# Moving the squares' sums, the sample copies and the row transposes at the border between attention and feed-forward

## The chip, the cores and the metric

The kernel runs on one core of one Trainium2 chip. The metric is the time of one execution in microseconds (us) on the device. Five engines work side by side, each through its own instructions in order: PE (matrix products), DVE (elementwise), ACT (activations and copies), POOL (elementwise) and SP (here only issuing transfers). Matrix products go to PSUM, from where ACT or DVE take them.

## The reference, cut to what matters

One decoder layer for two groups of tokens: 1024 prompt tokens and 8 x 4 sample tokens, width 1024, fp32.

```python
x = x + rms_norm(m, norm_g[1])                      # after the token mixer
h = rms_norm(x, norm_g[2])
x = x + rms_norm(mem_attend(h, mem_k, mem_v, *attn_w), norm_g[3])
h = rms_norm(x, norm_g[4])
x = x + rms_norm(swiglu(h, *ffn_w), norm_g[5])      # (silu(h @ w_gate) * (h @ w_up)) @ w_down
```

The border of this text is the third and fourth line: the attention's output projection, its norm (norm 3), the residual sum, and the norm of that (norm 4), from which the gate and up products start.

## The kernel before, in words

Activations are kept transposed: 128 features on the partitions, tokens along the free axis, in tiles of 128 x 2 x 264 (528 elements). Eight tiles (k = 0 to 7) are the 1024 features of one half of the tokens; the halves are called b = 0 and b = 1. Each fp32 operand is split into a high and a low part (ACT copies the high part, DVE subtracts to get the low part), and each product is three matmuls: high x high, high x low, low x high.

**Output projection** (`attn_out`): for a half, eight blocks, one for each 128 output features. A block is 24 pairs of matmuls (`pao`), then ACT squares the result from PSUM (`sq_n`), the square is added to a running sum (`square_sum`, lines 204 to 210), and ACT copies the result out of PSUM with its gain (`mg`, line 979). Only with both done is the block's PSUM tile free; there are three of them.

**Residual and norms** (`tokens_ffn`): a matmul with ones (`os_n`, line 216) adds the squares over the partitions, ACT takes the root (line 223), DVE the inverse (line 224). DVE scales the eight `mg` tiles by it and adds them to the eight residual tiles `xo` (line 81). Those are squared again and summed (`acc_n`), and with the second inverse the normed tiles (`a`, line 1255) are made and split. For b = 0 they are the matrices A11 and A12, for b = 1 DVE makes the sums and differences of a Strassen scheme (AS1 to AS4, A22). In the kernel before, norm 3's squares are added on POOL for both halves, norm 4's on POOL for b = 0 and on DVE for b = 1.

**Rows** (`rows_in`): each residual tile is also needed in row form at the end. PE transposes its four 128x128 pieces into PSUM (`xn`, line 1229), ACT copies them (line 1231) and SP stores them; the eight sample columns are copied to `xsam` by POOL (line 1225).

**Products ahead** (`ahead_pairs`): six pairs of gate and up blocks for b = 0. Each block is two half products of 12 pairs of matmuls (`xA`, line 1308), with A11 and then with A12; between the two ACT copies the first half's result (`p`, line 1330), which is stored. The gate block is activated by ACT (`gA`, line 1336), and DVE multiplies it by the up block. After these come the 11 full pairs.

A scheduler orders the instructions of each engine from the order of the code and its own estimate of time. What is written side by side with `run(...)` alternates, a step of each in turn. Rings of buffers couple the engines: two PSUM tiles for `xn` and `xA` together, eight tiles tagged `co` (`mg`, normed tiles, gates), five tagged `tmp` (squares, row copies, copies of products), two or four for each kind of weight buffer.

Of the kernel before, what the change touches and what calls it, by code (L numbers as in the profile page):

```python
# [12 lines left out]
AF = mybir.ActivationFunctionType  # L13
# [7 lines left out]
KT = 8  # L21
# [21 lines left out]
def decode_step(ctx: ExitStack, tc: tile.TileContext, I, O):  # L43
    nc = tc.nc
    act, dve, pool, pe, sync = nc.scalar, nc.vector, nc.gpsimd, nc.tensor, nc.sync
# [9 lines left out]
    def unit(name, dt=F32, shape=(P, 2, W), tag="act"):  # L55
        return acts.tile(list(shape), dt, tag=tag, bufs=BUFS[tag], name=name)

    def tmp(name, dt=F32, shape=(P, 2, W)):
        return unit(name, dt, shape, "tmp")
# [3 lines left out]
    def mm_tile(name):  # L63

        turn[0] += 1
        third = turn[0] % 3 == 0 and not streams
        return ps.tile([P, 2, 512], F32, tag="pw" if third else "mm", bufs=1 if third else 2, name=name)
# [12 lines left out]
    def tt(out, a, b, op, eng=None):  # L80
        (eng or dve).tensor_tensor(out, a, b, op)  # L81
# [4 lines left out]
    def split_into(hi, lo, x, scale=None, eng=None):  # L86

        if scale is None:
            act.activation(hi, x, AF.Copy)  # L89
            low(eng or dve, lo, x, hi)  # L90
        else:
            act.activation(hi, x, AF.Copy, scale=scale)
            dve.scalar_tensor_tensor(lo, x, scale, hi.bitcast(F32), op0=ALU.mult, op1=ALU.subtract)
# [6 lines left out]
    def run(*gens):  # L100

        gens = [g for g in gens if g is not None]
        while gens:
            gens = [g for g in gens if next(g, END) is not END]

    END = object()
# [53 lines left out]
    def gain(n, k):  # L160
        return gains[:, 8 * n + k: 8 * n + k + 1]
# [42 lines left out]
    def square_sum(acc, x, k, name, eng=None):  # L204
        if k == 0:
            act.activation(acc, x, AF.Square)
        else:
            sq = tmp(f"sq_{name}{k}")
            act.activation(sq, x, AF.Square)  # L209
            tt(acc, acc, sq, ALU.add, eng or pool)  # L210
# [9 lines left out]
    def rsqrt(x, n, name, r):  # L220

        for s, total in enumerate(ones_sum(x, name)):
            act.activation(r[:, s, :], total, AF.Sqrt, scale=1.0 / n, bias=eps_rms)  # L223
        dve.reciprocal(r, r)  # L224
        return r
# [34 lines left out]
    def rtile(name):  # L260
        return tiny.tile([P, 2, W], F32, tag="r", bufs=2, name=f"r_{name}")

    def acc_tile(name):
        return accp.tile([P, 2, W], F32, tag="acc", bufs=2, name=f"acc_{name}")
# [710 lines left out]
    def result(b, n, out, norm, acc):  # L975

        mg = unit(f"mg{norm}{b}{n}", tag="co")
        square_sum(acc, out, n, f"n{norm}{b}")
        act.activation(mg, out, AF.Copy, scale=gain(norm, n))  # L979
        return mg  # L980

# [28 lines left out]
    mgA, mgB = [], []  # L1010
    accA, accB = acc_tile("moA"), acc_tile("moB")
# [178 lines left out]
    xsam = fp.tile([P, KT, 4, NB], F32, name="xsam")  # L1190

    def fa_tile(name, dt=F32):
        return fp.tile([P, 2, W], dt, tag="fa", bufs=24, name=name)
# [19 lines left out]
    def keep(n, kt, x):  # L1213

        fa = n in ("S1", "S2", "S4")
        hi, lo = ((fa_tile if fa else unit)(f"A{n}{kt}{i}", F32R) for i in "hl")
        split_into(hi, lo, x)
        A[n][kt] = (hi, lo)

    xo = [[], []]  # L1220

    def rows_in(b, k):

        x = xo[b][k]
        pool.tensor_copy(xsam[:, k, 2 * b:2 * b + 2, :], x[:, :, 0:8])
        pt = mm_tile(f"xn{b}{k}")[:, 0].rearrange("p (t d) -> p t d", t=4)
        for s in range(2):
            for i in range(2):
                pe.transpose(pt[:, 2 * s + i], x[:, s, 8 + i * P:8 + (i + 1) * P], ident)
        xn = tmp(f"xn{b}{k}_", F32, (P, 4, P))  # L1230
        act.activation(xn, pt, AF.Copy)
        sync.dma_start(xnat[4 * b:4 * b + 4, :, k * P:(k + 1) * P].rearrange("t p d -> p t d"), xn)

    def tokens_ffn(b, mgs, acc):

        r = rsqrt(acc, D, f"n3{b}", rtile(f"n3{b}"))
        acc2 = acc_tile(f"n4{b}")
        yield
        for k in range(KT):
            name = f"xo{b}{k}"  # L1240
            if b and k == 7:
                x = fp.tile([P, 2, W], F32, name=name)
            else:
                x = unit(name) if b and k < 3 else fa_tile(name)
            sync.dma_start(x, xres[b][k])
            tt(mgs[k], mgs[k], r, ALU.mult)
            tt(x, x, mgs[k], ALU.add)
            square_sum(acc2, x, k, f"n4{b}", dve if b else pool)
            xo[b].append(x)
            yield  # L1250
        r2 = rsqrt(acc2, D, f"n4{b}", rtile(f"n4{b}"))

        def normed(k, name):
            t = unit(name, tag="co")
            dve.scalar_tensor_tensor(t, xo[b][k], gain(4, k), r2, op0=ALU.mult, op1=ALU.mult)
            return t

        for kt in range(4):
            if b == 0:
                for n, k in (("11", kt), ("12", kt + 4)):  # L1260
                    t = normed(k, f"a{n}{kt}")
                    keep(n, kt, t)
                    sync.dma_start(hb0[k], t)
            else:
                a11, a12 = (unit(f"b1{i}{kt}", tag="co") for i in range(2))
                sync.dma_start(a11, hb0[kt])
                sync.dma_start(a12, hb0[kt + 4])
                a21, a22 = normed(kt, f"a21{kt}"), normed(kt + 4, f"a22{kt}")
                s3 = unit(f"s3{kt}", tag="co")
                tt(s3, a11, a21, ALU.subtract)  # L1270
                tt(a21, a21, a22, ALU.add)
                tt(a11, a21, a11, ALU.subtract)
                keep("S2", kt, a11)
                keep("S1", kt, a21)
                keep("S3", kt, s3)
                tt(a12, a12, a11, ALU.subtract)
                keep("S4", kt, a12)
                keep("22", kt, a22)
            yield


# [2 lines left out]
    def raw_tile(name, shape):  # L1284
        wturn[0] += 1
        if wturn[0] % 2:
            return ring.tile(list(shape), F32, tag="wst", name=name)
        return fp.tile(list(shape), F32, tag="ww", bufs=2, name=name)
# [14 lines left out]
    def product(out, w, a, first=True):  # L1303
        outs = [out[0], out[1]]
        for kt in range(4):
            for i, (c, x) in enumerate(((0, 0), (0, 1), (1, 0))):
                for o, part in zip(outs, both):
                    pe.matmul(o, lhsT=w[:, c, kt], rhs=part(a[kt][x]), start=first and kt == 0 and i == 0,  # L1308
                              stop=kt == 3 and i == 2, skip_group_check=not first)

    def x_tile(name):
        t = ps.tile([P, 2, 512], F32, tag="mm", bufs=2, name=name)
        return t[:, :, :W], [t[:, 0, :W], t[:, 1, :W]]
# [5 lines left out]
    def ahead_pairs():  # L1319

        for i in range(AHEAD):
            g = None
            for m in range(2):
                src = mats[m][0, :, 256 * i:256 * i + P].rearrange("(k p) n -> p k n", p=P)
                ww = raw_tile(f"wA{i}{m}", (P, KT, P))
                sync.dma_start(ww, src)
                X, xs_ = x_tile(f"xA{i}{m}")
                product(xs_, two_parts(ww[:, 0:4], f"wA{i}{m}a"), A["11"])
                p1 = tmp(f"p1{i}{m}")
                act.activation(p1, X, AF.Copy)  # L1330
                sync.dma_start(p1d[i][m], p1)
                yield
                product(xs_, two_parts(ww[:, 4:8], f"wA{i}{m}b"), A["12"], False)
                if m == 0:
                    g = unit(f"gA{i}", tag="co")
                    act.activation(g, X, AF.Silu)
                else:
                    tt(g, g, X, ALU.mult)
                    sync.dma_start(hidd[2 * i][0], g)
                yield  # L1340
# [69 lines left out]
    mgA, mgB = [], []  # L1410
    accA, accB = acc_tile("aoA"), acc_tile("aoB")
# [6 lines left out]
    run(first)  # L1418
    run(second)
    streams.append(1)  # L1420

    def all_rows():
        for b in range(2):
            for k in range(KT):
                while len(xo[b]) <= k:
                    yield
                rows_in(b, k)
                yield

    run(tokens_ffn(1, mgB, accB), ahead_pairs(), all_rows())  # L1430
    for i in range(PAIRS):
        pair(i)
    streams.clear()
# [87 lines left out]
    for s4 in range(4):  # L1521
        b, s = s4 // 2, s4 % 2
# [44 lines left out]
```

## Time and profile before

| | us |
|---|---|
| median of 3 runs | 1656.31 |
| lowest, highest | 1650.68, 1656.35 |
| the profiled execution | 1651.99 |
| its span | 1650.3 |

Busy time in the profiled execution: PE 1509.9 us (91%), DVE 997.2 (60%), ACT 684.5 (41%), POOL 352.0 (21%). Engine shares are means over stages with different limits; the border lies between about 757 and 980 us. A row of a time-ordered view gives the start, the duration, the engine, the line, the operation with output and inputs, and in brackets the time that the engine stood still just before with the instruction that released it. Several equal instructions in a row are one row (x2, x4), and then the duration is that of all of them.

### The profile page before, as it was taken

The page shows a single profiled execution, that of the slowest core. Times are in us where ns is not written, and L with a number is a line of the kernel's source. Part 1 is how long each engine was busy: PE and PEld are TensorE (multiplying, and loading weights), DVE is VectorE, ACT ScalarE, POOL GpSimd, SP SyncE. Part 2 cuts the span into 40 slices and gives each one's busy share as a digit, 9 for nine tenths or more (in the row PEclk, how much of TensorE's full clock was granted, in tenths as well). Part 3 has the DMA queues.
Part 4 walks back from the last instruction along what each step waited for, and adds up shares of the span by engine and source line. Part 5 has one row for each costly group of instructions (what it writes and reads, how often), then busy time and mean ns, then how long its engine had stood idle before and what let it go on. Part 6 is the DMA issues. An engine that isn't in the chain of part 4 may idle for free. (4 is left out here: it accounts for less than half of the span.)

```text
span 1650.3 us, 29329 instructions
## 1 busy us (share of the span) xinstructions
PE 1509.9 (91%) x11731; PEld 1460.7 (89%) x11731; DVE 997.2 (60%) x1678; ACT 684.5 (41%) x1226; POOL 352.0 (21%) x436
## 2 busy tenths in 40 slices
PE   7998889889999899789958799999999999999995
PEld 5888878889999889679957799999999999999995
DVE  6888786476468845583555857766555533444345
ACT  5444533457554544474444633232333334212122
POOL 1366556330334320051342000000000000000004
PEclk9989989899999999899979989999999999999998
DMA  8422223456244503546335643332222225232124
GB/s 244 148 72 69 64 70 100 137 163 197 71 144 149 175 25 117 156 152 190 88 103 177 198 149 117 117 115 93 84 78 78 69 92 173 91 105 66 52 65 156
DMA packets 216116, 194.33 MB, mean 118 GB/s; under 512 B 21900, under 2 KB 180036, under 8 KB 215972
## 3 DMA queue, kind: packets, MB, share of 16 engines
q1 hardware_dynamic: 215852, 192.30, 37.9%
q8 instruction: 92, 1.51, 0.4%
q14 instruction: 44, 0.36, 0.1%
q10 hardware_dynamic: 128, 0.16, 0.0%
HBM read 146.33 MB, written 46.51 MB: 117 GB/s over the span
## 5 line engine op out<-in xcount | busy, mean ns | idle before, releaser
L1496 POOL COPY ysam<-ya 128x8 f32<-128x8 f32 x32 | 5.6, 192 | 717.9 <-DVE ya L81 717.7
L81 DVE TENSOR_TENSOR ya<-ya,fd 128x528 f32<-128x528 f32 x64 | 45.0, 704 | 105.8 <-PE fd L191 105.8
L191 PE MATMUL pao<-oth,hi_wa 128*128 128x264 f32 x256 | 54.9, 297 | 19.1 <-ACT mg L979 19.1
L176 ACT ACTIVATE hi_wd<-st_wd 128x1024 fp32r<-128x1024 f32 x20 | 21.2, 1060 | 121.5 <-PE fd L191 121.3
L81 DVE TENSOR_TENSOR c<-c,X 128x528 f32<-128x528 f32 x51 | 35.8, 703 | 39.7 <-PE X L1308 39.7
L191 PEld LDWEIGHTS pao<-oth,hi_wa 128*128 128x128 f32 x256 | 42.0, 199 | 19.9 <-ACT mg L979 19.7
L191 PE MATMUL pao<-oth,lo_wa 128*128 128x264 f32 x256 | 54.4, 294 | 0.4 <-DVE lo_wa L84 0.4
L191 PE MATMUL pao<-otl,hi_wa 128*128 128x264 f32 x256 | 54.1, 294 | 0.0
L643 PE MATMUL pcv<-vf,cm 128*128 128x128 f32 x320 | 46.2, 296 | 8.4 <-ACT ob L645 5.0
L643 PEld LDWEIGHTS pcv<-vf,cm 128*128 128x128 f32 x320 | 42.8, 209 | 10.5 <-issue 6.2
L84 DVE TENSOR_TENSOR lo_wa<-st_wa,hi_wa 128x1024 fp32r<-128x1024 f32 x16 | 20.6, 1288 | 47.3 <-ACT hi_wa L176 47.3
L191 PEld LDWEIGHTS pao<-oth,lo_wa 128*128 128x128 f32 x256 | 41.7, 197 | 0.7 <-DVE lo_wa L84 0.6
L191 PEld LDWEIGHTS pao<-otl,hi_wa 128*128 128x128 f32 x256 | 41.8, 198 | 0.1
L84 DVE TENSOR_TENSOR kl<-pkr,kh 128x512 fp32r<-128x512 f32 x32 | 21.9, 690 | 28.8 <-ACT kh L89 28.6
L84 DVE TENSOR_TENSOR lo_wd<-st_wd,hi_wd 128x1024 fp32r<-128x1024 f32 x20 | 24.5, 1225 | 22.9 <-ACT hi_wd L176 19.8
L81 POOL TENSOR_TENSOR acc_n<-acc_n,sq_n 128x528 f32<-128x528 f32 x21 | 29.5, 1406 | 39.6 <-ACT sq_n L209 39.5
L224 DVE RECIPROCAL r_n<-r_n 128x528 f32<-128x528 f32 x8 | 27.6, 3451 | 15.7 <-ACT r_n L223 15.7
L753 DVE TENSOR_TENSOR_SCAN M<-rho,X 128x256 f32<-128x256 f32 x32 | 29.8, 956 | 7.3 <-POOL X L81 7.3
L89 ACT ACTIVATE wc<-t 128x512 fp32r<-128x512 f32 x22 | 13.9, 632 | 47.5 <-PE X L1308 25.4
L645 ACT ACTIVATE ob<-pcv,cbias 128x128 f32<-128x128 f32 x32 | 11.6, 364 | 48.9 <-PE pcv L643 47.8
L81 DVE TENSOR_TENSOR c<-c,c 128x528 f32<-128x528 f32 x45 | 31.6, 702 | 0.1
L89 ACT ACTIVATE kh<-pkr 128x512 fp32r<-128x512 f32 x32 | 18.9, 597 | 30.7 <-PE pkr L1135 28.7
(2045 smaller groups left out, 5726.6 us busy)
## 6 DMA issues: line engine op xcount, KB each, us to landing
hr<-hid SPq DMA_DIRECT2D x44, 264.0 KB
ww<-in_w_gate_dram SPq DMA_DIRECT2D x22, 512.0 KB
ww<-in_w_up_dram SPq DMA_DIRECT2D x22, 512.0 KB
st_wd<-in_w_down_dram SPq DMA_DIRECT2D x20, 512.0 KB
hid<-c SPq DMA_DIRECT2D x38, 264.0 KB
xo<-x SPq DMA_DIRECT2D x32, 264.0 KB
kr<-in_cache_mem_k_dram SPq DMA_DIRECT2D x32, 256.0 KB
st_wo<-in_w_out_dram SPq DMA_DIRECT2D x16, 512.0 KB
```

Of the source, the lines that this page charges most:

```text
L81: (eng or dve).tensor_tensor(out, a, b, op)
L84: eng.tensor_tensor(lo, x, hi.bitcast(F32), ALU.subtract)
L89: act.activation(hi, x, AF.Copy)
L176: act.activation(hi[:, :cols], stv, AF.Copy)
L191: pe.matmul(out, lhsT=a, rhs=part(b), start=first and i == 0, stop=last and i == 2)
L224: dve.reciprocal(r, r)
L643: pe.matmul(o, lhsT=cm[:, d].rearrange("p c t -> p (c t)"), rhs=vf[:, g, 4 - d:CH - d], start=d == 0, stop=d == 4)
L645: act.activation(ob[:, g4], o, AF.Identity, bias=cbias[:, gg:gg + 1])
L753: dve.tensor_tensor_scan(out=M[:, i], data0=rho[:, pair:pair + 1].to_broadcast([P, 256]), data1=X[:, i], initial=0.0, op0=ALU.mult, op1=AL ...
L1496: pool.tensor_copy(ysam[:, n, 2 * b + s, :], yacc[b][n][:, s, 0:8])
```

## The change

Norm 4's squares are added on DVE for both halves, and norm 3's on DVE for the last two blocks of each half. The sample columns are copied by ACT in place of POOL. The row transposes of b = 0 stand ahead of the products, those of b = 1 inside the loop that makes its normed tiles. The products are no longer alternated evenly with the residual and the rows: the residual of b = 1 advances one step for each step of the products, and two steps of products are taken once its eight tiles are done.

```diff
-        square_sum(acc, out, n, f"n{norm}{b}")
+        square_sum(acc, out, n, f"n{norm}{b}", dve if norm == 3 and n > 5 else pool)
...
-        pool.tensor_copy(xsam[:, k, 2 * b:2 * b + 2, :], x[:, :, 0:8])
+        act.activation(xsam[:, k, 2 * b:2 * b + 2, :], x[:, :, 0:8], AF.Copy)
...
-            square_sum(acc2, x, k, f"n4{b}", dve if b else pool)
+            square_sum(acc2, x, k, f"n4{b}", dve)
...
                 keep("22", kt, a22)
+                rows_in(1, kt)
+                rows_in(1, kt + 4)
             yield
...
-    def all_rows():
-        for b in range(2):
-            for k in range(KT):
-                while len(xo[b]) <= k:
-                    yield
-                rows_in(b, k)
-                yield
-
-    run(tokens_ffn(1, mgB, accB), ahead_pairs(), all_rows())
+    for k in range(KT):
+        rows_in(0, k)
+    chain, fill = tokens_ffn(1, mgB, accB), ahead_pairs()
+    for n in range(KT + 5):
+        next(chain, END)
+        for _ in range(2 if n > KT else 1):
+            next(fill, END)
+    run(chain)
+    run(fill)
```

The order of PE at the sum of norm 4's squares of b = 0 (`os_n` from `acc_n`), in the second half's output projection, before:

```order
L191 MATMUL pao_9661<-oth_7975,lo_wa_9658 128x264 x2
L191 MATMUL pao_9661<-oth_7977,hi_wa_9657 128x264 x2
L191 MATMUL pao_9661<-otl_7978,hi_wa_9657 128x264 x2
L216 MATMUL os_n_9527<-acc_n_9238,ones 128x264
L216 MATMUL os_n_9529<-acc_n_9238,ones 128x264
L191 MATMUL pao_9661<-oth_7977,lo_wa_9658 128x264 x2
L191 MATMUL pao_9661<-oth_7979,hi_wa_9657 128x264 x2
```

and with the change:

```order
L191 MATMUL pao_9601<-otl_7978,hi_wa_9597 128x264 x2
L191 MATMUL pao_9601<-oth_7977,lo_wa_9598 128x264 x2
L191 MATMUL pao_9601<-oth_7979,hi_wa_9597 128x264 x2
L191 MATMUL pao_9601<-otl_7980,hi_wa_9597 128x264
L216 MATMUL os_n_9527<-acc_n_9238,ones 128x264
L216 MATMUL os_n_9529<-acc_n_9238,ones 128x264
L191 MATMUL pao_9601<-otl_7980,hi_wa_9597 128x264
L191 MATMUL pao_9601<-oth_7979,lo_wa_9598 128x264 x2
```

The sum moved from the sixth block (9661, after 17 of its 24 pairs) to the fifth (9601, after 19 and a half).

The order of PE where the second half's output projection (`pao_9781` is its last block) meets the first product, before:

```order
L1308 MATMUL xA_9846<-A113l,wA00a 128x264 x2
L1308 MATMUL xA_9846<-A113h,wA00a 128x264 x2
L1229 MATMUL xn_9878<-ident,xo_9239 128x128 x4
L216 MATMUL os_n_9836<-acc_aoB,ones 128x264
L216 MATMUL os_n_9838<-acc_aoB,ones 128x264
L1308 MATMUL xA_9846<-A120h,wA00b 128x264 x2
```

and with the change:

```order
L191 MATMUL pao_9781<-oth_7981,lo_wa_9778 128x264 x2
L1229 MATMUL xn_9836<-ident,xo_9239 128x128 x4
L1229 MATMUL xn_9845<-ident,xo_9244 128x128 x4
L216 MATMUL os_n_9908<-acc_aoB,ones 128x264
L216 MATMUL os_n_9910<-acc_aoB,ones 128x264
L1229 MATMUL xn_9854<-ident,xo_9251 128x128 x4
L1229 MATMUL xn_9863<-ident,xo_9258 128x128 x4
L1229 MATMUL xn_9872<-ident,xo_9265 128x128 x4
L1229 MATMUL xn_9881<-ident,xo_9272 128x128 x4
L1229 MATMUL xn_9890<-ident,xo_9279 128x128 x4
L1229 MATMUL xn_9899<-ident,xo_9286 128x128 x4
L1310 MATMUL xA_9918<-A110h,wA00a 128x264 x2
```

All eight row transposes of b = 0 and the sum of norm 3's squares of b = 1 (`os_n` from `acc_aoB`) now stand ahead of the first product; before, one transpose stood behind each half product. Behind it the half products of the first two pairs now come as gate, up, gate, up (A11, A11, A12, A12).

On ACT, the copy that frees the fourth block's PSUM tile (`mg_9590`) had only splits of normed tiles ahead of it; before:

```order
L89 ACTIVATE A121h<-a_9555 128x528
L89 ACTIVATE A112h<-a_9562 128x528
L89 ACTIVATE A122h<-a_9569 128x528
L979 ACTIVATE mg_9590<-pao_9477,gains 128x528
L89 ACTIVATE A113h<-a_9576 128x528
```

and with the change:

```order
L89 ACTIVATE A112h<-a_9562 128x528
L89 ACTIVATE A122h<-a_9569 128x528
L89 ACTIVATE wA10a<-wA_10066 128x512
L89 ACTIVATE wA11a<-wA_10142 128x512
L979 ACTIVATE mg_9590<-pao_9477,gains 128x528
L89 ACTIVATE A113h<-a_9576 128x528
```

The two copies of weights of the second pair, which stood three rows further ahead, now stand directly ahead of it.

## Rows read from the trace of the kernel before

**Rows 1.** Busy time by stretch: PE, PEld, DVE, ACT, POOL, granted clock, DMA share, GB/s.

```profile
806.00:873.00 67.00, 47.90 (x351) 47.05 (x350) 40.09 (x46) 29.22 (x47) 25.64 (x21) 0.85 0.32 100
873.00:953.50 80.50, 61.71 (x456) 57.09 (x454) 61.34 (x88) 45.82 (x81) 8.37 (x9) 0.92 0.61 185
...
980.00:1240.00 260.00, 260.00 (x2142) 260.00 (x2142) 168.57 (x261) 85.22 (x141) 0.00 (x0) 1.00 0.34 106
```

**Rows 2.** Waits of PE, 806 to 960: total us, times, longest.

```profile
PE pao L191 <- ACT mg L979: 19.1, 3, 14.1
PE xn L1229 <- ACT gA L1336: 10.2, 2, 6.1
PE xA L1308 <- ACT p L1330: 1.9, 5, 0.8
PE xA L1308 <- ACT xn__10482 L1231: 1.4, 1, 1.4
```

**Rows 3.** PE in order of time at the border.

```profile
805.67 1.05 PE L216 MATMUL os_n<-acc_aoA,ones 128*128 128x264 f32 x4
...
830.04 0.81 PE L191 MATMUL pao<-oth,hi_wa 128*128 128x264 f32 x2 [4.74 <-ACT mg L979]
...
842.57 1.05 PE L216 MATMUL os_n<-acc_n,ones 128*128 128x264 f32 x4
...
859.38 0.81 PE L191 MATMUL pao<-oth,hi_wa 128*128 128x264 f32 x2 [14.06 <-ACT mg L979]
...
872.67 0.41 PE L1308 MATMUL xA<-A110h,wA00a 128*128 128x264 f32 x2
...
875.60 0.60 PE L1229 MATMUL xn<-ident,xo 128*128 128x128 f32 x4
...
951.68 1.12 PE L1229 MATMUL xn<-ident,xo 128*128 128x128 f32 x4 [0.69 <-ACT xn__10637 L1231]
953.48 0.81 PE L1308 MATMUL xA<-A110h,wA40a 128*128 128x264 f32 x2 [0.69 <-ACT xn__10675 L1231]
...
958.44 0.40 PE L1308 MATMUL xA<-A113h,wA40a 128*128 128x264 f32 x2
```

**Rows 4.** ACT in order of time, 815 to 966.

```profile
825.73 0.64 ACT L209 ACTIVATE sq_n<-xo 128x528 f32<-128x528 f32 x1 [2.98 <-POOL acc_n L81]
...
855.07 0.63 ACT L89 ACTIVATE wA10a<-wA 128x512 fp32r<-128x512 f32 x1 [1.52 <-DMA wA<-in_w_gate_dram]
...
858.63 0.70 ACT L979 ACTIVATE mg<-pao,gains 128x528 f32<-128x528 f32 x1
...
887.84 0.64 ACT L206 ACTIVATE acc_n<-xo 128x528 f32<-128x528 f32 x1 [2.78 <-DVE xo L81]
```

**Rows 5.** DVE in order of time, 755 to 966.

```profile
822.75 1.22 DVE L84 TENSOR_TENSOR lo_wa<-st_wa,hi_wa 128x1024 fp32r<-128x1024 f32 x1
...
844.17 3.45 DVE L224 RECIPROCAL r_n<-r_n 128x528 f32<-128x528 f32 x1 [3.48 <-ACT r_n L223]
...
849.63 1.21 DVE L84 TENSOR_TENSOR lo_wa<-st_wa,hi_wa 128x1024 fp32r<-128x1024 f32 x1
...
919.19 3.45 DVE L224 RECIPROCAL r_n<-r_n 128x528 f32<-128x528 f32 x1 [1.96 <-ACT r_n L223]
...
955.28 0.70 DVE L84 TENSOR_TENSOR AS43l<-b,AS43h 128x528 fp32r<-128x528 f32 x1
```

**Rows 6.** POOL by line, 817 to 848: busy us, mean ns, idle before.

```profile
L81 POOL TENSOR_TENSOR acc_n<-acc_n,sq_n 128x528 f32<-128x528 f32 x7 | 9.1, 1306 | 0.1
...
L1225 POOL COPY xsam<-xo 128x16 f32<-128x16 f32 x8 | 7.6, 987 | 13.7 <-DVE xo L81 13.7
```

**Rows 7.** The nearest small copy on ACT, by line, 100 to 960.

```profile
L743 ACT ACTIVATE wsam<-pw 128x16 f32<-128x16 f32 x13 | 2.3, 177 | 7.6 <-PE pw L742 7.6
```

**Rows 8.** PE after transposes alone, near the program's start, in order of time.

```profile
28.71 0.81 PE L191 MATMUL pu<-h00h,hi_wi 128*128 128x264 f32 x2
...
33.27 0.44 PE L191 MATMUL pu<-h03l,hi_wi 128*128 128x264 f32 x2
```

## The prediction

> **What bounds the kernel now.** I read the stretches of the span first [rows 1]. Before and after the border TensorE (PE) is the conveyor: from 980 to 1240 us it is busy 260.00 of 260.00 us at granted clock 1.00. What is late at 980 is late at the end, and nothing there can give time back or take more. In the border PE is busy 47.9 of 67 us and then 61.7 of 80.5, at mean clocks 0.85 and 0.92. So the change is worth what it does to the start of the last eight half products, at 953.48 us [rows 3]; from there the order on PE is the same in both kernels.
>
> PE's waits come next [rows 2], then PE in order of time [rows 3]. Two waits are large. Block 7 of the second half's output projection (the blocks of 24 pairs of matmuls are called 1 to 8) starts at 859.38 after 14.06 us without work: it needs the PSUM tile of block 4, which ACT's scaled copy frees only from 858.63 on [rows 4]. And 10.2 us are lost before row transposes, waiting for the gate activation on ACT, which stood behind the square of the second half's first residual tile, itself late from DVE (887.84, [rows 4]). Block 5 waits 4.74 us until 830.04.
>
> Why is ACT late for block 4? Its scaled copy needs one of eight tiles that the first half's normed tiles hold, and stands on ACT behind their splits. That chain begins with the sum of squares of the first half. POOL adds it: 7 adds of 1306 ns beside 8 sample copies of 987 ns mean [rows 6]. Only when they are done can PE sum over partitions (842.57), ACT take the root, DVE invert it (844.17 to 847.6, [rows 5]).
>
> **The change part by part.** I work from the profiled execution, 1651.99 us (1.7 of it outside the span of 1650.3); the median of the runs shown is 4.3 above it, the lowest 1.3 below.
>
> *First sum of squares, last two adds on DVE.* PE reaches the partition sum at 805.67 by its own order [rows 3], and the root needs nothing else: worth 0. The two DVE adds (0.70 us each, the length of the last row of [rows 5]) are taken while DVE waits for the root.
>
> *Second sum on DVE, copies on ACT.* DVE is through its residual adds and a weight split at 822.75 + 1.22 = 823.97 [rows 5]. Four adds of 0.70, which overlap a little (0.63 apart), end at 826.5. ACT's sixth square, which waited for POOL to free a tile at 825.73 [rows 4], now waits for the first DVE add, 824.65. Behind it stand a weight copy that needs block 4's matmuls off PE (825.4 to 826.4), two squares, and the copy that frees PSUM for block 5: 828.1. Block 5 starts 1.9 us earlier, at 828.15. The remaining adds stand behind the next split on DVE and end at 829.6. The partition sum stood behind 17 pairs of block 6 and now stands behind 19.5 pairs of block 5. With PE slow for 11 pairs after its wait (953.48 to 958.44 shows 11 pairs in 4.96 us, [rows 3]) and 0.244 us a pair after that (12 in the 2.93 us from 872.67 to 875.60), 19.5 pairs take 7.0: it runs at 835.2, not 842.57.
>
> Inverse: 5.05 us later as before (842.57 to 847.62), 840.25. Then on DVE one split of 1.2, five normed tiles of 0.7, a low part, and the split for block 8: 846.8. Only then can SP issue the load of the next gate weight into that buffer, and two copies of this weight now stand on ACT directly ahead of block 4's copy. Before, the same split ended at 850.84 and ACT had the weight at 855.07 [rows 4, 5]: 4.2 us. So 851.0, and with two copies and the scaled copy (0.6 + 0.5 + 0.7) 852.8. Block 7 starts at 852.9 instead of 859.38: **6.5 us gained**, and block 8 ends at 866.2 where it ended at 872.67.
>
> The small copies on ACT, eight in each half, have no row of their own; the nearest are a plain copy of the same 128x16 at 177 ns [rows 7] and, from above, a 128x512 copy at 0.63 us (855.07, [rows 4]). In the first half they lie where ACT waits for DVE or PE anyway: 0, at most 8 x 0.63 = 5.0. In the second half five of them stand ahead of the gate activation: 0.9 to 3.2 us of ACT, of which up to 2.5 would be seen. I take the 177, the same shape, and nothing on the path.
>
> Where POOL and DVE both read, the trace shows the sample copies stretched to 987 ns mean [rows 6]. The Trainium skill, "SBUF — State Buffer", section "Who interferes with whom", says that a DVE instruction with two SBUF inputs and a POOL instruction that reads SBUF exclude each other, and the later waits for the whole of the earlier one. By that rule the moved adds can still meet three POOL adds of the other sum, so up to 3.9 us: they end at 833.5, not 829.6. Against 835.2 that is free; if PE keeps its clock over the shorter wait (the partition sum is then reached at 832.9) it would take 0.6 of the 2.3 won. No run here shows which comes first.
>
> *Row transposes of the first half at one place.* Eight groups of four transposes now stand alone between block 8 and the first product. Two PSUM tiles serve them, each emptied by ACT. Bounds: 8 x 0.60 = 4.8 us if nothing waits (875.60), 8 x 1.81 = 14.5 if each waits for the one before (951.68 to 953.48), plus 0.7 for a partition sum. I take 9.7: two in flight halve the 1.81 (7.2), 0.7, and 1.8 because the sixth to eighth reuse a tile whose store must have landed, with the next weight loads queued beside it. After transposes alone PE is slow: after those at the start of the program, matmul pairs begin 0.44 apart from 28.71 to 33.27 [rows 8], ten of them 2.1 us late; I add that.
>
> *Two pairs of products interleaved, second residual earlier.* In place of wait, product, transposes, product the order is gate, up, gate, up: each evacuation has a product of 2.93 us to hide in. The inverse for the second half no longer stands behind a product's copies, and the gate activation that cost 6.1 us now has a product more of time. From block 8 to the last eight half products the matmuls are the same: 80.8 us before (872.67 to 953.48), of which 16 x 2.93 + 16 x 0.44 (four transposes, 0.60 long with the last one's tail) + 1.4 = 55.3 is work and 25.5 waiting or slow. After: 5.5 in the transposes (9.7 less 3.5 work less 0.7), 2.1 slow, 0.3 for each of four products that still wait for a copy (1.2), 4.8 in the eight products that keep transposes between them (the second half's, as before: three waits for a row copy of at most 1.4 and three for a product's copy of 0.4 mean, [rows 2]), 1.3 at the last: 14.9. **10.6 us gained.** And without a wait of 4 us ahead of them, the last products begin at full clock: 4.96 - 11 x 0.244 = **2.3 gained**.
>
> Sum: 6.5 + 10.6 + 2.3 = 19.4; 1651.99 - 19.4 = 1632.6, and 1633 with rounding. A run like the median would read 4 more.
>
> **Rivals.** *DVE ends last.* From the second inverse at 919.19 to the last low part at 955.28 + 0.7 DVE never rests [rows 5], and ACT's copies that free PSUM stand among its products. By my sum the inverse moves to 907.3 (866.2 + 9.7 + 9 x 2.93 + 3.3 + 0.7 and 1 for the root), 11.9 earlier; if DVE's 36.8 us set the start of the last products, only that is won: 1640. For it: DVE is as full as PE there. Against: the copies that free PSUM stand earlier among its products than before, with about 2.7 us in hand.
>
> *The long wait stays.* Weight load and eight stores of normed tiles meet on the DMA queue; if the load takes 6 us longer, block 7 starts at 859 and 6.5 is lost: 1639. Against: ACT waited 1.52 for it before (855.07), with stores of normed tiles in flight too.
>
> *Nothing at the end.* The last products start earlier but wait for their weights or for the second half's matrices, and the time is back to within 8 us of before, about 1648 to 1655. Against: 260.00 of 260.00 busy means there was slack in all that follows.
>
> *The stores set the pace (slower).* Five temporary tiles serve the row copies, their stores, the products' copies and the squares. Eight stores now come in a row, and ACT stops in order at each. At s us per store the last lands 3 + 8s after block 8; the gate activation behind them is due at 20 us. Each us beyond s = 2.1 costs 8 us; from s = 4.6 on the 19.4 are eaten, and at 6 the time is 1651.99 - 19.4 + 31 = 1664. Before, with a product between two of these stores, the wait cannot show. Against: 256 KB each, and the stretch from 873 on moved 185 GB/s on average [rows 1], which makes s 1.4.
>
> **How the numbers follow.** Forecast 55% (1626 to 1641), DVE ends last 20% (1640), long wait stays 10% (1639), nothing 10% (1648 to 1655), stores 5% (1664). The range: at the fast end, transposes in 5.5 us (-4.2), no slow pairs in either place (-4.4): 1624, less 1.3 for the runs' spread, 1623. At the slow end, transposes at 15.2 (+5.5) and copies at 0.63 (+2.5), or DVE last (+7.5), plus 4.3 if the runs lie where the median did, 1645; 1646 with the 0.6 of the adds. About 0.5% (8 us) is what a measurement of this kernel tells from no change. Below 1648 lie the first three cases and a little of the fourth: faster 0.87; within 0.5% 0.08; slower 0.05.
>
> **What would show it.** Right: block 5's wait under 3.5 us; the partition sum inside block 5 near 835; block 7's wait near 10 us; the first product about 10 us after block 8, its first pairs 0.44 apart; no wait over 2 us between there and the last eight half products, which begin near 936 at full pace; from there a copy of before. Wrong: ACT standing at the sixth to eighth row copy for several us, a wait of PE on DVE's gate product or on the gate activation, or a new wait after 960.

## The result, and the profile after

The changed kernel takes 1629.57 us (median of 4 runs, 1627.53 to 1633.35) against 1653.7 us for the kernel before on the same chip (median of 4 runs): a ratio of 0.9857, 95% interval 0.9828 to 0.9887. The forecast was 1633, range 1623 to 1646. The profiled executions took 1651.99 and 1629.99 us; their spans, 1650.3 and 1628.3, differ by 22.0.

PE in order of time after the change (columns as in [rows 3]), from the first partition sum on:

```profile
803.25 1.05 PE L216 MATMUL os_n<-acc_aoA,ones 128*128 128x264 f32 x4
...
825.47 0.51 PE L191 MATMUL pao<-oth,hi_wa 128*128 128x264 f32 x2 [2.57 <-ACT mg L979]
...
831.06 1.16 PE L216 MATMUL os_n<-acc_n,ones 128*128 128x264 f32 x4 [0.57 <-DVE acc_n L81]
...
849.46 0.81 PE L191 MATMUL pao<-oth,hi_wa 128*128 128x264 f32 x2 [10.28 <-ACT mg L979]
...
863.46 0.60 PE L1229 MATMUL xn<-ident,xo 128*128 128x128 f32 x4
...
873.95 0.51 PE L1310 MATMUL xA<-A110h,wA00a 128*128 128x264 f32 x2 [2.54 <-ACT xn__9895 L1231]
...
933.50 0.51 PE L1310 MATMUL xA<-A110h,wA40a 128*128 128x264 f32 x2 [0.77 <-ACT xn__10646 L1231]
...
956.95 0.41 PE L1310 MATMUL Z<-AS10h,wd 128*128 128x264 f32 x2
```

The last row is the first full pair; before, it stands here, and the last eight half products ran at a mean granted clock of 0.91 (columns of the second fence as in [rows 1]):

```profile
979.11 0.41 PE L1308 MATMUL Z<-AS10h,wd 128*128 128x264 f32 x2
```

```profile
953.48:979.11 25.63, 25.63 (x193) 25.63 (x193) 10.13 (x18) 8.53 (x16) 0.00 (x0) 0.91 0.32 108
```

The first partition sum itself, which both programs reach by the same work, stands at 805.67 before and 803.25 after; over the profiles of this study, one of each kernel, it lies anywhere from 800.33 to 808.36. What comes ahead of it is therefore left out, and everything is counted from it:

| us after the first partition sum | before | predicted | after |
|---|---|---|---|
| block 5 starts | 24.37 | 22.48 | 22.22 |
| partition sum of norm 4 | 36.90 | 29.53 | 27.81 |
| block 7 starts | 53.71 | 47.23 | 46.21 |
| block 8 ends | 67.00 | 60.53 | 60.21 |
| first product starts | 67.00 | 70.23 | 70.70 |
| last eight half products start | 147.81 | 130.71 | 130.25 |
| first full pair starts | 173.44 | 154.04 | 153.70 |
| from there to the end of the span | 671.19 | 671.19 | 671.35 |

The border gave 19.74 us of the 22.0, the stretch ahead of it 2.42, and the end took 0.16 back. By stretch (columns as in [rows 1]) the kernel after has:

```profile
803.25:863.46 60.21, 46.38 (x350) 45.28 (x348) 47.29 (x54) 28.93 (x55) 10.86 (x5) 0.91 0.34 108
863.46:933.50 70.04, 60.06 (x458) 56.72 (x456) 56.24 (x80) 44.85 (x86) 0.00 (x0) 0.98 0.68 209
933.50:956.95 23.45, 23.45 (x192) 23.45 (x193) 15.76 (x26) 10.19 (x19) 0.00 (x0) 1.00 0.45 143
957.00:1218.00 261.00, 261.00 (x2149) 261.00 (x2149) 169.51 (x261) 86.03 (x142) 0.00 (x0) 1.00 0.35 107
```

From 957 to 1218 PE is again never idle, as in the last of [rows 1]. Of PE's waits from 757 to 965 (view as in [rows 2]) the gate activation has gone, and one large one is left:

```profile
PE pao L191 <- ACT mg L979: 13.3, 3, 10.3
PE xA L1310 <- ACT xn__9895 L1231: 2.5, 1, 2.5
PE xA L1310 <- ACT xn__10420 L1231: 1.3, 1, 1.3
...
PE xn L1229 <- ACT xn__9886 L1231: 0.8, 1, 0.8
```

ACT in order of time shows why block 7 still waits, and what the eight row copies wait for (columns as in [rows 4]):

```profile
847.67 0.63 ACT L89 ACTIVATE wA10a<-wA 128x512 fp32r<-128x512 f32 x1 [1.61 <-DMA wA<-in_w_gate_dram]
848.21 0.61 ACT L89 ACTIVATE wA11a<-wA 128x512 fp32r<-128x512 f32 x1
848.73 0.68 ACT L979 ACTIVATE mg<-pao,gains 128x528 f32<-128x528 f32 x1
...
870.11 0.60 ACT L1231 ACTIVATE xn__9886<-xn 128x512 f32<-128x512 f32 x1 [0.90 <-DMA xnat<-xn__9841]
873.30 0.60 ACT L1231 ACTIVATE xn__9895<-xn 128x512 f32<-128x512 f32 x1 [2.60 <-DMA xnat<-xn__9850]
```

### The profile page after: what moved, and what is told of

Same layout as the page of the kernel before. It is cut to its first block, busy times and chain, and to the rows that moved or that the text cites. A ratio compares the mean times of both kernels' runs of the same rounds, so it can differ in the third digit from the quotient of the medians.

```text
span 1628.3 us, 29327 instructions
## 1 busy us (share of the span) xinstructions
PE 1501.8 (92%) x11731; PEld 1454.1 (89%) x11731; DVE 1004.9 (62%) x1689; ACT 685.6 (42%) x1242; POOL 327.6 (20%) x409
## 5 line engine op out<-in xcount | busy, mean ns | idle before, releaser
L191 PEld LDWEIGHTS pao<-oth,hi_wa 128*128 128x128 f32 x256 | 40.9, 194 | 15.2 <-ACT mg L979 13.9
L84 DVE TENSOR_TENSOR lo_wa<-st_wa,hi_wa 128x1024 fp32r<-128x1024 f32 x16 | 19.4, 1214 | 34.0 <-ACT hi_wa L176 34.0
L1385 ACT ACTIVATE c<-Z 128x528 f32<-128x528 f32 x22 | 13.5, 612 | 41.4 <-PE Z L1310 41.4
```

Source lines behind the costliest of these rows:

```text
L84: eng.tensor_tensor(lo, x, hi.bitcast(F32), ALU.subtract)
L191: pe.matmul(out, lhsT=a, rhs=part(b), start=first and i == 0, stop=last and i == 2)
L1385: act.activation(c22, Z[:, :, :W], AF.Copy)
```

## The experiments

The theory is the prediction's: the early sum frees block 4's tile and with it block 7, the new order of rows and products removes the waits behind block 8, and the two add up. The rivals: one part does it all, or a wait further on takes the gain back. Each profile is read by the same PE rows as above, counted from the first partition sum; ratios are to the kernel before on the same chip, with the 95% interval. The gain by the ratio and the gain in the last column agree to within 4 us, except for e (18.7 us by the ratio, 13.91 in the column), so as a gain in time a column of one profile is good to a few us.

| run | ratio | norm-4 sum | block 8 ends | last eight start | first full pair |
|---|---|---|---|---|---|
| before | 1 | 36.90 | 67.00 | 147.81 | 173.44 |
| changed | 0.9857 (0.9828 to 0.9887) | 27.81 | 60.21 | 130.25 | 153.70 |
| a: sums and copies | 0.9965 (0.9948 to 0.9982) | 28.57 | 59.63 | 140.72 | 166.35 |
| b: sums | 0.9961 (0.9942 to 0.9980) | 28.58 | 59.50 | 142.35 | 167.17 |
| c: copies | 0.9998 (0.9981 to 1.0016) | 34.54 | 65.57 | 146.91 | 172.73 |
| d: rows and order | 0.9912 (0.9888 to 0.9937) | 36.52 | 66.46 | 136.51 | 159.97 |
| e: rows between products | 0.9887 (0.9866 to 0.9908) | 28.59 | 59.68 | 136.10 | 159.53 |
| f: row copies in other ring | 0.9838 (0.9824 to 0.9853) | 27.82 | 60.14 | 125.47 | 148.93 |
| g: 4 normed tiles in other ring | 0.9846 (0.9811 to 0.9882) | 28.57 | 56.06 | 125.76 | 149.22 |
| h: 8 normed tiles in other ring | 0.9777 (0.9755 to 0.9799) | 28.58 | 48.52 | 115.31 | 138.78 |
| i: h and 8 row copies | 0.9817 (0.9790 to 0.9845) | 27.81 | 47.86 | 118.36 | 141.82 |
| j: all sums on DVE | 0.9884 (0.9852 to 0.9917) | 29.58 | 62.16 | 132.60 | 156.08 |
| k: h and 4 row copies | 0.9822 (0.9798 to 0.9846) | 28.58 | 48.53 | 120.15 | 143.60 |
| l: d and 8 normed tiles | 0.9899 (0.9878 to 0.9921) | 36.95 | 51.26 | 130.65 | 154.09 |

**a. Sums and copies alone** (the kernel before with these lines of the change):

```diff
-        square_sum(acc, out, n, f"n{norm}{b}")
+        square_sum(acc, out, n, f"n{norm}{b}", dve if norm == 3 and n > 5 else pool)
-        pool.tensor_copy(xsam[:, k, 2 * b:2 * b + 2, :], x[:, :, 0:8])
+        act.activation(xsam[:, k, 2 * b:2 * b + 2, :], x[:, :, 0:8], AF.Copy)
-            square_sum(acc2, x, k, f"n4{b}", dve if b else pool)
+            square_sum(acc2, x, k, f"n4{b}", dve)
```

> The kernel before with only the squares' sums on DVE and the sample copies on ACT; rows and order of the products stay. Theory (the parts add up): counted from the partition sum of the first half's norm-3 squares, block 7 starts 46 us after it (before 53.7, with the whole change 46.2), block 8 ends 60 us after it (67.0, 60.2); from there to the last eight half products 81 us as before, in slow pairs at their start; about 7 us faster, 1647. Rival (the border takes it back): the gate activation and the second inverse set the start of the last products, and the stretch behind block 8 grows by 4 us or more; within 3 us of before.

Measured: 7.09 us at the first full pair. Block 7 starts at 46.06, and behind block 8 the stretch to the last products is 81.09 as before (80.81), then 25.63 as before. The theory holds. Its waits from 855 to 945 still show both waits for the gate activation, 5.8 and 4.2 us:

```profile
PE xn L1229 <- ACT gA L1336: 9.9, 2, 5.8
```

**b. Sums alone** (the first and third line pairs of a).

> Only the squares' sums on DVE; the sample copies stay on POOL. Theory: the sum is what was late, and POOL's copies alone cost DVE's adds little: partition sum of norm 4 inside block 5, about 28 us after the first partition sum (before 36.9), block 7 at 46 to 48, 5 to 7 us faster. Rival (what POOL reads holds DVE): the eight copies and the adds hold each other up, the partition sum waits 3 us or more on DVE, and block 7 starts no earlier than 50 us after the first sum; 0 to 3 us faster.

Measured: 6.27 us; the partition sum at 28.58 waits for nothing. The rival falls in this place: POOL's copies did not make DVE's adds late enough to matter. The adds even end 1.1 us earlier than in a (26.59 for 27.71), since POOL, still busy with its copies, came to its own adds later. With the copies still on POOL the longer of the two gate waits is 6.66 us instead of 5.79.

**c. Copies alone** (the second line pair of a).

> Only the sample copies on ACT; the sums stay on POOL. Theory: seven adds of 1.31 us without the copies between them end 7 us earlier, but the partition sum on PE stands only some 9 pairs of matmuls further ahead, so it moves by 2 to 3 us, block 7 with it; 2 to 3 us faster. Rival: the copies are the whole of it, block 7 starts 46 us after the first sum, 7 us faster.

Measured: the partition sum comes 2.4 us earlier, block 7 2.25, but at the first full pair only 0.71 us are left: 0.82 go in blocks 7 and 8 (14.11 us for the two instead of 13.29), 0.72 behind them. By time no difference. The theory had the sum right and the end too high by 1 to 2 us; the rival falls. b and c add up to 6.98, a gave 7.09.

**d. Rows and order alone** (the changed kernel with the lines of a undone).

> Only the rows at their new places and the products in their new order; sums and copies stay on POOL. Theory: block 7 starts 53.7 us after the first sum as before; block 8 to the last eight half products takes 70 us in place of 80.8, and those run at full pace (23.5 us for 25.6): 13 us faster, 1639 to 1641. Rival: without the earlier sum the stretch stays bound by the gate activation and the inverse on DVE, less than 7 us faster.

Measured: 13.47 us. Block 8 to the last eight half products takes 70.05, those 23.46. The theory holds. a and d together would be 20.56; the whole change gave 19.74.

**e. The first half's rows back between the half products**, everything else as changed:

```diff
-    for k in range(KT):
-        rows_in(0, k)
...
             next(fill, END)
+        if n < KT:
+            rows_in(0, n)
```

> The changed kernel with the first half's row transposes again one behind each half product; sums, copies and the residual's advance as changed. Theory (the rows ahead are what frees the second PSUM tile, so that two products can alternate): without it the products stand alone again and wait for their copies and the gate activation; from the first partition sum to the first full pair 163 to 166 us (changed 153.7, with sums and copies alone 166.4), some 10 us slower than the changed kernel. Rival (the residual's advance did it): 155 to 158 us, within 4 us of the changed kernel.

Measured: 159.53, 5.8 us behind the changed kernel and between the two, so neither number is met. From block 8 to the last products it takes 76.42 us, where a takes 81.09 and the changed kernel 70.04. Its waits show what each half of the edit is for:

```profile
PE xn L1229 <- ACT gA L1338: 5.7, 1, 5.7
```

Of the two waits for the gate activation in a, the 4.2 us one has gone with the steady residual and the second half's rows at their new place; the 5.8 us one stays, and is gone in d and the changed kernel, where the first half's rows stand ahead and the products alternate.

**f. The row copies of the first half in another ring**, changed kernel:

```diff
-        xn = tmp(f"xn{b}{k}_", F32, (P, 4, P))
+        xn = tmp(f"xn{b}{k}_", F32, (P, 4, P)) if b else fp.tile([P, 4, P], F32, tag="fa", bufs=24, name=f"xn{b}{k}_")
```

> The changed kernel with the first half's eight row copies written to tiles of another ring, so that none waits for a store. Theory (the stores cost what ACT shows, 0.9 and 2.6 us): the stretch between block 8 and the first product shrinks from 10.5 to 7 or 8 us, and the last eight half products start 2.5 to 3.5 us earlier, counted from the first partition sum; 3 us faster than the changed kernel. Rival (hidden anyway): the next wait, for DVE's sums or the weights, takes it back before the last eight half products; within 1 us of the changed kernel.

Measured: the transposes' stretch shrinks from 10.49 to 7.13 us, and the last products start 4.78 us earlier. PE waits 0.20 us where it waited 2.54:

```profile
869.82 0.51 PE L1310 MATMUL xA<-A110h,wA00a 128*128 128x264 f32 x2 [0.20 <-ACT xn__9895 L1231]
```

The theory holds, at a little more than its size: besides 3.36 us in the transposes there are 1.4 us more up to the last products: no pair of the first product runs slow (12 pairs in 3.03 us, 4.55 with the change), and the mean clock (863 to 928) is 1.00, not 0.98. In this profile 2.6 us are lost again far behind the border, where PE waits 1.8 us for a copy in the down projection; the runs put it 0 to 3 us ahead of the changed kernel, which a measurement of this kernel cannot tell.

**g. Four of the first half's normed tiles in the other ring**, changed kernel:

```diff
-            t = unit(name, tag="co")
+            t = fa_tile(name) if not b and k % 4 < 2 else unit(name, tag="co")
```

> The changed kernel with four of the first half's eight normed tiles in another ring, so that block 4's scaled copy finds a free tile before them. Theory (block 7's wait is only that tile): block 7's wait falls from 10.3 to under 2 us, block 8 ends 50 to 52 us after the first partition sum (60.2), and all of it arrives: first sum to first full pair 144 to 146 us (153.7), 8 to 9 us faster than the changed kernel. Rival (the normed tiles and their splits are needed next): the first product or ACT's row copies wait instead, and only 3 to 4 us arrive.

Measured: block 7 no longer waits, but the wait has moved on by one block, to block 8, since block 5's scaled copy meets the same shortage:

```profile
850.52 0.81 PE L191 MATMUL pao<-oth,hi_wa 128*128 128x264 f32 x2 [5.03 <-ACT mg L979]
```

4.15 us are won at block 8's end and 4.48 at the first full pair. That the tile was what block 4's copy waited for is shown; the size is near the rival's 3 to 4, though not for its reason.

**h. All eight** (the condition is `if not b`).

> As the run before, with all eight normed tiles in the other ring. Theory: block 7 waits for nothing, and the end is the same as with four, 144 to 146 us, since the same normed tiles are needed for the first product. Rival: with the four scaled copies ahead of the splits on ACT, the splits and with them the first product come later, 2 us or more slower than with four.

Measured: block 8 ends 11.7 us earlier than with the change alone, and 14.9 us arrive at the first full pair: 138.78. This is better than the theory's 144 to 146 and the fastest version of the study, 1619.04 us (median of 4 runs, 1614.89 to 1621.79), which beats both kernels. PE's waits from 806 to 935:

```profile
PE pao L191 <- ACT mg L979: 3.0, 2, 2.6
PE xn L1229 <- ACT mg L979: 1.6, 1, 1.6
PE xA L1310 <- ACT xn__10420 L1231: 1.3, 1, 1.3
...
```

and its stretches: clock 0.96 and then 1.00 to the end of the border, where the changed kernel has 0.91 and 0.98.

```profile
803.19:851.71 48.52, 45.41 (x349) 44.52 (x348) 44.00 (x50) 27.59 (x53) 8.59 (x5) 0.96 0.44 145
851.71:918.50 66.79, 58.50 (x458) 55.30 (x457) 58.91 (x85) 45.91 (x88) 0.00 (x0) 1.00 0.75 228
```

The theory had left out two things. No pair of blocks 7 and 8 runs slow when no wait stands ahead of them, and block 8 ends at 48.52, not at the 50 to 52 named for g. And 3.2 us more are won behind block 8: 1.9 in the transposes (8.61 for 10.49), the rest in the first product, which is at full pace as in f.

**i. Normed tiles and row copies in the other ring** (f and h together).

> The changed kernel with all eight normed tiles and all eight row copies of the first half in the other ring. Theory (two waits, one behind the other): block 8 ends 48.5 us after the first partition sum as with the normed tiles alone, and the store waits of ACT (2.3 and 0.7 us there) go too: first sum to first full pair 134 to 136 us (138.8 with the normed tiles alone, 153.7 with the change as it is). Rival (the ring of 24 is now the limit: the second half's residual tiles are loaded only when the row transposes free theirs): the residual and with it the second inverse come later, 139 us or more.

Measured: 141.82, worse than h by 3.0. The residual's last loads are issued at 863.10 and 864.95 (h: all by 848.3), and the second inverse starts 89.6 us after the first partition sum (h: 86.0). But PE shows another wait as the largest, which run k was made to tell apart.

**j. All squares of norm 3's second half on DVE too**, changed kernel:

```diff
-        square_sum(acc, out, n, f"n{norm}{b}", dve if norm == 3 and n > 5 else pool)
+        square_sum(acc, out, n, f"n{norm}{b}", dve if norm == 3 and (b or n > 5) else pool)
```

> The changed kernel with the second half's norm-3 squares added on DVE too, so that POOL adds nothing at the border. Theory (DVE and POOL held each other up): the last three adds of the first half's norm-4 squares, 5.34 us with the change, take 2 us, and each add of the other sum 0.70 us on DVE for 1.3 to 4.2 on POOL; the partition sum waits for nothing; the end stays within 1 us of the changed kernel, since DVE takes five adds more. Rival (the adds waited for their squares from ACT): the three adds take 4 us or more as before.

With the change, DVE's last three adds took 5.34 us; here each add takes 0.70 on DVE. First the changed kernel, DVE and POOL, then this run, DVE:

```profile
825.66 5.34 DVE L81 TENSOR_TENSOR acc_n<-acc_n,sq_n 128x528 f32<-128x528 f32 x3
```

```profile
824.90 5.54 POOL L81 TENSOR_TENSOR acc_aoB<-acc_aoB,sq_n 128x528 f32<-128x528 f32 x3 [35.40 <-ACT sq_n L209]
```

```profile
823.21 0.70 DVE L81 TENSOR_TENSOR acc_n<-acc_n,sq_n 128x528 f32<-128x528 f32 x1
823.83 0.70 DVE L81 TENSOR_TENSOR acc_aoB<-acc_aoB,sq_n 128x528 f32<-128x528 f32 x1
824.45 0.70 DVE L81 TENSOR_TENSOR acc_n<-acc_n,sq_n 128x528 f32<-128x528 f32 x1
```

In the changed kernel the adds of both engines lay side by side; without POOL's, each of DVE's takes 0.70 us, so it was POOL's that drew them out, and the rival falls. But the end is 2.4 us later, not within 1: the partition sum stands further back in block 5 (29.58), a weight split is placed ahead of the inverse, and block 7 waits 11.55 us.

**k. Normed tiles and only four row copies in the other ring** (run i, with this condition):

```diff
-        xn = tmp(f"xn{b}{k}_", F32, (P, 4, P)) if b else fp.tile(...)
+        xn = tmp(f"xn{b}{k}_", F32, (P, 4, P)) if b or k > 3 else fp.tile(...)
```

> All eight normed tiles and the first four row copies in the other ring, the last four row copies in the ring of five; the 20 tiles and the second half's four fit into 24, so the residual's loads need not wait for transposes. Theory (the late residual loads were what the run before lost): first sum to first full pair 134 to 137 us, 2 to 4 us faster than with the normed tiles alone (138.8). Rival (the products' order, which here starts the second gate product before the first up product is whole, waits for the gate activation whatever the loads do): 139 us or more.

Measured: 143.60, so the rival's number. The premise of the theory failed, however: the last four loads of the residual still went out late, between the row stores on SP (857 to 866). What decides between the two is PE's wait itself. In h the order is gate, up, gate, up; here, in i and in l the second gate product stands ahead of the first up product's second half, and needs the PSUM tile that the first gate activation frees. The row of k:

```profile
872.88 0.81 PE L1310 MATMUL xA<-A110h,wA10a 128*128 128x264 f32 x2 [3.16 <-ACT gA L1338]
```

The wait is 3.16 us in all three, and ACT fills it in the same way in all three: a weight copy, which can start only when the first gate product has left PE, a square, a load of the activation's table, and the activation. The square is the first of the second half's residual, but it does not stand waiting for it. In k:

```profile
869.76 0.63 ACT L89 ACTIVATE wA20b<-wA 128x512 fp32r<-128x512 f32 x1 [2.31 <-PE xA L1310]
870.29 0.63 ACT L206 ACTIVATE acc_n<-xo 128x528 f32<-128x528 f32 x1
870.93 1.28 ACT L1338 ACT_TABLE_LOAD   x1
872.22 0.61 ACT L1338 ACTIVATE gA<-xA 128x528 f32<-128x528 f32 x1
```

From the first product to the last eight it takes 63.17 us in i, 64.18 in k and 63.23 in l, against 58.18 in h. Counted from the first product, l's late loads (872.67 to 877.09) go out some 5.5 us earlier than i's (863.10 to 867.82), and the stretch is the same; PE waits for no residual tile in any of the three. So the late loads show no cost here. The order costs 5 to 6 us, for the most part the 3.16 and the slow pairs behind them; i wins back 1.9 ahead of the first product, which is how it ends 3.0 behind h.

**l. The change without sums and copies, normed tiles in the other ring** (d and h).

> All eight normed tiles in the other ring, rows and products in the new order, but sums and sample copies on POOL as before. Theory (the early sum was worth what it freed block 4's tile by, and now that tile is free anyway): block 7 waits under 2 us, block 8 ends 50 to 52 us after the first partition sum (48.5 with the early sum), first sum to first full pair 140 to 142 us (138.8): sums and copies are worth 2 to 3 us here, not 7. Rival (the normed tiles themselves are needed): the first product waits for the last split of a normed tile, 145 us or more, and the sums are worth their 7 us still.

Measured: the first half of the theory holds. Block 8 ends at 51.26, only 2.7 us behind h: once block 4's copy has its tile, the early sum is worth no more there. The second half falls: 154.09, 15.3 behind h. The rival's number is passed, but not by its mechanism. Of the 15.3, 2.7 are there at block 8's end, 7.6 come in the transposes and 5.0 behind the first product, from the products' order as in i. In the transposes PE waits 6.26 us for the second half's norm-3 sum, whose last add on POOL took 7.37 us while DVE worked through ten splits without a pause (859.80 to 865.98):

```profile
867.19 2.13 PE L216 MATMUL os_n<-acc_aoB,ones 128*128 128x264 f32 x4 [6.26 <-POOL acc_aoB L81]
```

```profile
859.77 7.37 POOL L81 TENSOR_TENSOR acc_aoB<-acc_aoB,sq_n 128x528 f32<-128x528 f32 x1 [5.08 <-ACT sq_n L209]
```

So with that ring opened, the last two adds of norm 3 on DVE, which the prediction had weighed for the first half only, guard against a wait that the kernel before does not show. This is read from the rows: l leaves out all sums and copies at once, and no run leaves out these adds alone.

## Why the prediction was right, point by point

- **First sum of squares: worth 0.** Right. The sum stands at 800.33 to 806.72 with the edit and at 803.13 to 808.36 without it, but the difference lies ahead: from the first pair of the first half's output projection to the sum PE takes 59.5 to 60.3 us with it and 59.7 to 60.1 without.
- **Block 5, 1.9 us earlier.** 2.15, and so in a and b (22.21, 22.22); without the sums on DVE it is 24.37 (d).
- **Partition sum at 835.2** (29.53 counted from the first). Measured 27.81. The step that failed is the pace: 11 slow pairs were charged after block 5's wait, and in this profile none came (its first pairs begin 0.24 to 0.35 us apart). It then waited 0.57 us for DVE's last add, which ended at 831.00, or 833.42 on the time scale of the kernel before. By the rule of the Trainium skill ("SBUF — State Buffer", section "Who interferes with whom") the prediction had estimated 833.5 for it, and a wait of 0.6 should PE keep its clock. The trace agrees, and j takes the effect away by taking POOL's adds away.
- **Block 7, 6.5 us gained.** 7.50 by its start and 6.79 by block 8's end, because 11 of its pairs ran slow where 8 did before. The wait is 10.28 (forecast: near 10), with the two weight copies directly ahead of block 4's copy and 1.61 us for the load (1.52 before, [rows 4]). From the split that frees its buffer (842.45) to the weight on ACT (847.67) it took 5.2 us where 4.2 was charged; the rival that this load comes 6 us later falls, with 1.0 of its 6 seen.
- **Small copies on ACT: nothing.** They took 204 ns each (177 was taken from [rows 7]). Moving them off POOL gave 0.7 to 0.8 us in the profiles (c, and a against b), no more than the slow pairs differ from one profile to the next, and nothing by the runs (c 0.9998; a 0.9965 against b 0.9961).
- **Transposes, 9.7 us.** 10.49, bounds 5.5 to 15.2. ACT stood 0.90 and 2.60 us at the sixth and seventh copy, for stores, where 1.8 was charged. f shows that these waits are real and on the path: taking them away gives 4.78 us. So the slower rival had its mechanism right and its size wrong.
- **Slow pairs after the transposes, 2.1 us.** Right in size: the fourth to eleventh pair begin some 0.44 us apart (874.78 to 878.22), 8 x 0.20 = 1.6 us.
- **No wait over 2 us among the products, 10.6 gained behind block 8.** 10.77 gained; the longest waits, of 0.77 to 1.30, are for copies of the second half's rows, as priced (1.4). The first pairs of the last products are 0.24 apart and their stretch 23.45: **2.3 at full clock** came as 2.18.
- **The rival that DVE ends last.** It falls: the second inverse stands 101.0 us after the first partition sum (forecast 101.6), and PE waits for no DVE row behind it. **The rival of nothing at the end** falls too: 671.19 and 671.35.

The sum was 19.4; the border gave 19.74. That it comes so close is partly luck. Up to block 8 the partition sum was 1.7 us early and the split behind the inverse 1.9, but the weight load took 1.0 more and the pairs of blocks 7 and 8 another 0.7, which left 0.3. Behind block 8 the transposes took 0.8 more and the products 0.9 less. The large waits came where the prediction had them. The 3.4 us by which the median beats the forecast are for the most part the 2.42 us ahead of the first partition sum, where the change has no part that the rows show.

## What to carry to other kernels

A wait that a late sum seems to cause can hang on a ring of buffers in between: the sum's 9 us earlier were worth 7 only because the scaled copy needed a tile that the normed tiles made from that sum held, and giving the normed tiles a ring of their own was worth twice as much on top of it (h). Work that stands between two products on the in-order engine does more harm by taking the second accumulator than by its own time (e); gather it in one place, and give what it writes as many buffers as it has pieces (f). Compare two profiles from a common row just ahead of the change, and not from the span's start.

## What the runs showed of the hardware that was not expected

- The same wait does not always bring the slow clock. Block 5 starts after about 2.6 us without work (2.57 in the changed kernel, 2.58 in a) in all kernels that have the early sum. In the profiles of the changed kernel, f and i its pairs keep to the full pace (granted clock 1.00 from 825.5 to 829.5 in the changed kernel) and the partition sum stands at 27.81 to 27.82. In those of a, b, e, g, h and k seven to nine pairs begin 0.44 us apart (0.57 from 822.5 to 826.5 in a, a mean of slow pairs at 0.50 and full ones) and it stands at 28.57 to 28.59; j has such pairs too. What the slow pairs after this short wait cost was thus 0 or 0.8 us from one profile to the next.
- An add of 128x528 on POOL, 1.29 us at its shortest in l, lasted 7.37 us there beside ten back-to-back DVE splits, and held PE for 6.26 us. An engine with little to do can still be the late one.
- Between the square and the gate activation ACT loads a table for 1.28 us (870.93 in k, 888.49 in the kernel before). It is part of the 6.1 us that the prediction put down to the late square, and no sum here had it as a term.
